# Splitting attention and delta-rule weights with casting and adding DMAs, and adaLN products of attention on VectorE, in a two-layer hybrid decoder

## The chip, the cores and the metric

One core of a Trainium2 chip runs the kernel. The metric is the device time of one execution in microseconds (us). The engines are TensorE (PE, with its weight loads shown apart as PEld), VectorE (DVE), ScalarE (ACT), GpSimd (POOL) and SyncE (SP). Each engine runs its own queue of instructions strictly in order, so an instruction that waits holds up everything behind it on its engine. DMAs are issued by SP, ACT or POOL, each from its place in that engine's queue.

## The reference

What is computed, for 512 positions of width 1024 and two layers:

```python
cond = silu(c)
for layer in range(2):
    mod = cond @ ada_w[layer] + ada_b[layer]
    shift_m, scale_m, gate_m, shift_f, scale_f, gate_f = split(mod, 6)
    h = rmsnorm(x, norm_mix_g[layer]) * (1 + scale_m) + shift_m
    if layer % 2 == 0: mixed = attention_head_groups(h, positions, attn_w_in, attn_w_out)
    else:              mixed = gated_deltanet(h, gdn_w_in, conv_w, a_log, dt_bias, norm_g, gdn_w_out)
    x = x + gate_m * mixed
    h = rmsnorm(x, norm_ffn_g[layer]) * (1 + scale_f) + shift_f
    x = x + gate_f * ((silu(gate) * up) @ ffn_w_out[layer])   # gate, up = split(h @ ffn_w_in[layer])
return rmsnorm(x, final_norm_g)
```

Attention has 8 block-sparse softmax heads with rotary positions and 8 stick-breaking heads, all of 64 columns. The gated delta rule has 8 heads of 128 columns: a short convolution on q, k and v, a triangular system solved in each chunk, and a scan over chunks.

## The kernel before

Everything is float32. A large product is made from three passes of TensorE: weight and activation are each split into a high part, rounded to the type fp32r, and a low part, the rest; the product is high by high, plus high by low, plus low by high. So every weight tile of 128x1024 floats (512 KB) must be split before TensorE can use it.

`fetch` loads the next tile of a fixed list (`weight_plan`) and splits it. SP issues the load into one of three buffers called `raw`; then `split` (lines 246 to 251) writes `wh`, the rounded copy, and `wl = raw - wh`. A letter in the plan names the engines: "a" copies on ACT and subtracts on DVE, "p" copies on ACT and subtracts on POOL, "g" copies on POOL and subtracts on DVE. There are two buffers each of `wh` and `wl`. `load_w` asks for tiles two ahead of the one in use. A projection tile feeds 24 matmuls of 512 columns; two tiles of the projection z of the delta rule feed 48 matmuls of 256 columns in each of two passes.

The letters before: attention's 12 tiles of q and k projections (`EA`) "g"; its four tiles of v (`EVA`) "a"; of the delta rule, k (`EK`) "g", q and v (`EQ`, `EV`) "p", the first half of z (`EZ`) "p" and the second half (`EZ2`) "g".

adaLN: a column of `mod` is the sum of a row tile `aw` (128x1024, loaded by SP into two buffers) times `cond`. With `AENG = "g"` the 24 tiles that fall into attention (`ADA`, six with each of the first four heads) are multiplied on POOL (line 211) and summed on ACT (line 212). All others are one instruction of DVE (line 214).

A scheduler orders the instructions of all engines from dependencies and its own estimate of durations; the program text sets priorities only. The stages follow one another: start with the first projections (0 to 62 us), attention with the other projections between its heads (62 to 313), output projection and first feed-forward (313 to 718), the delta rule (718 to 1050), second feed-forward (to the end). In the delta rule, POOL gathers diagonal blocks (`UC`), writes them to DRAM and reads them back in another shape (`dr1`), DVE inverts them in 31 steps (lines 991 and 993, tiles `DT` and `vp`), and POOL moves the result back the same way (`dr2`); then TensorE finishes the inverse (lines 1016 to 1041) among the matmuls of z (lines 1096 to 1098), and the scan follows.

Of the kernel before, what the change touches and what calls it, by code (L numbers as in the profile page):

```python
# [8 lines left out]
F32 = mybir.dt.float32  # L9
F32R = mybir.dt.float32r  # L10
BF16 = mybir.dt.bfloat16
I32 = mybir.dt.int32
AF = mybir.ActivationFunctionType
OP = mybir.AluOpType
# [46 lines left out]
NEARLY = 14  # L61
LATE = (3, 1)
ORDER = (0, 4, 1, 5, 2, 6, 3, 7)
EK, EQ, EV, EZ, EZ2 = 'g', 'p', 'p', 'p', 'g'
EA, EVA = 12 * 'g', 'aa'
NL = (2, 1)
OG, NG = (6, 8), 18
GS = 4
ROT = 2
NPOOL = 2  # L70
AENG = "g"
ADA = (6, 6, 6, 6, 0, 0, 0, 0)
NSPLIT = 4
NFIRST = 2
NFIRST_GDN = 2


def weight_plan(I):

    p = []

    def add(key, src, kc=KC, n=128, eng="a", keep=False):
        p.append((key, src, kc, n, eng, keep))

    def out(name, src, nsplit, parts, keep, spare=()):
        order = list(range(KC - nsplit)) + (1 if keep or spare else 2) * list(range(KC - nsplit, KC))
        for n in order:  # L90
            for a, b in parts:
                add((name, n, a), src[n][:, a:b], b - a,
                    keep="h" if n in spare else keep and n >= KC - nsplit)

    def ffn(l):
        first = [j + f for f in range(NFIRST) for j in (0, FC)]
        for j in first + [j + f for f in range(NFIRST, FC) for j in (0, FC)]:
            add(("ffn_in", l, j), I["ffn_in"][l, j], keep=j in first)
        out(("ffn_out", l), I["ffn_out"][l], NL[l], ((0, 8), (8, 16), (16, 22)), False, (7,) if l else ())

    def vproj(name, i, eng="a"):
        for j in (0, 4):
            add((name, i, j), I[name][i][:, j:j + 4], 4, 256, eng)

    for k in range(KC):
        add(("attn_first", k), I["attn_first"][k])
    vproj("attn_v", 0, EVA[0])
    vproj("attn_v", 1, EVA[1])
    for i in range(12):
        add(("attn_in", i), I["attn_in"][i], eng=EA[i])  # L110
    out("attn_out", I["attn_out"], NSPLIT, ((0, 8),), True)
    ffn(0)
    first = list(range(8, 8 + NFIRST_GDN))
    for i in 2 * first + list(range(8 + NFIRST_GDN, 16)):
        add(("gdn_in", i), I["gdn_in"][i], eng=EK)
    for i in range(8):
        add(("gdn_in", i), I["gdn_in"][i], eng=EQ)
    for i in range(16, 24):
        add(("gdn_in", i), I["gdn_in"][i], eng=EV)
    for i in range(4):  # L120
        vproj("gdn_z", i, EZ)
    for i in range(4):
        vproj("gdn_z", i, EZ2)
    for i in range(2):
        for n in range(KC):
            add(("gdn_out", n, 0), I["gdn_out"][n])
    ffn(1)
    return p


def build(nc, tc, I, O):
    V, G, A, PE = nc.vector, nc.gpsimd, nc.scalar, nc.tensor
    from contextlib import ExitStack
    ctx = ExitStack()
    with ctx:
        const = ctx.enter_context(tc.tile_pool(name="const", bufs=1))
        res = ctx.enter_context(tc.tile_pool(name="res", bufs=1))
        wpool = ctx.enter_context(tc.tile_pool(name="wpool", bufs=1))
# [104 lines left out]
        def split(src, h, l, eng="a"):  # L243
            ins = None
            if eng in "ap":
                ins = A.activation(h, src, AF.Copy)  # L246
            elif eng == "g":
                G.tensor_scalar(h, src, 1.0, 1.0, op0=OP.mult, op1=OP.mult)  # L248
            else:
                V.tensor_copy(h, src)  # L250
            (G if eng == "p" else V).tensor_tensor(l, src, h.bitcast(F32), op=OP.subtract)  # L251
            return ins


        plan = weight_plan(I)
        loaded, dmas, spare = [], [], []
        used = [0]
        ahead = [0]
        kctx = [None]
        kpool = [None]  # L260
# [3 lines left out]
            kpool[0] = kctx[0].enter_context(tc.tile_pool(name="keep", bufs=1, side="right", reuse_waits="tile"))  # L264


        def fetch():
            _, dram, kc, n, eng, keep = plan[len(loaded)]
            raw = wpool.tile([128, kc, n], F32, name="raw", tag="raw", bufs=3)
            dmas.append(nc.sync.dma_start(raw, dram).ins)  # L270
            if keep == "h":

                w = [[], []]
                for j in range(0, kc, 4):
                    m = min(4, kc - j)
                    t = [x.rearrange("p (a b) -> p a b", b=n)[:, :m] for x in spare.pop(0)]
                    split(raw[:, j:j + m], *t, eng)
                    for i in range(2):
                        w[i] += [t[i][:, k:k + 1] for k in range(m)]
                loaded.append(w)  # L280
                return
            pool, bufs = (kpool[0], 4) if keep else (wpool, 2)
            h = pool.tile([128, kc, n], F32R, name="wh", tag="wh", bufs=bufs)
            l = pool.tile([128, kc, n], F32R, name="wl", tag="wl", bufs=bufs)
            split(raw, h, l, eng)
            loaded.append((h, l))

        def load_w(key):
            i = used[0]
            assert plan[i][0] == key, (plan[i][0], key)  # L290
            while len(loaded) < min(i + 1 + ahead[0], len(plan)):
                fetch()
            used[0] += 1
            w, loaded[i] = loaded[i], None
            return w
# [215 lines left out]
def attention(e, x0ctx):  # L511
    nc, tc, V, G, A, PE, I = e.nc, e.tc, e.V, e.G, e.A, e.PE, e.I
    from contextlib import ExitStack
    with ExitStack() as ctx:
# [271 lines left out]
        for p in range(4):  # L786
            qa, ka, qb, kb = cur
            for h in range(2):
                steps.append([])
                moba(p, h, qa, ka)  # L790
                for j in range(sum(ADA[:2 * p + h]), sum(ADA[:2 * p + h + 1])):
                    with tc.issue_after(e.dmas[KC - 1]), tc.issue_after(sin[1].ins):
                        e.ada(0, 2 + j // 8, j % 8, eng=AENG[j % len(AENG)])
                stick(p, h, qb, kb)
# [495 lines left out]
```

## Time and profile before

| | us |
|---|---|
| median of 3 runs | 1452.05 |
| lowest and highest run | 1450.31, 1454.83 |
| the profiled execution | 1451.28 |
| its span in the profile | 1449.4 |
| PE busy | 1392.6 |
| DVE busy | 879.5 |
| ACT busy | 583.2 |
| POOL busy | 403.6 |

The profiled execution is 1.9 us longer than its span and 0.8 us shorter than the median. A busy time is the sum of an engine's instructions in the profile; instructions that wait, branch or issue DMAs are not in it. A group's row gives its line, engine, operation and tiles, how often it ran, its busy time and the mean of one, and the idle time just before it with what ended it. PEclk is the clock granted to TensorE as a share of its full 2.4 GHz; the other level is half of that.

### The profile page before, as it was taken

The page shows a single profiled execution, that of the slowest core. Times are in us where ns is not written, and L with a number is a line of the kernel's source. Part 1 is how long each engine was busy: PE and PEld are TensorE (multiplying, and loading weights), DVE is VectorE, ACT ScalarE, POOL GpSimd, SP SyncE. Part 2 cuts the span into 40 slices and gives each one's busy share as a digit, 9 for nine tenths or more (in the row PEclk, how much of TensorE's full clock was granted, in tenths as well). Part 3 has the DMA queues.
Part 4 walks back from the last instruction along what each step waited for, and adds up shares of the span by engine and source line. Part 5 has one row for each costly group of instructions (what it writes and reads, how often), then busy time and mean ns, then how long its engine had stood idle before and what let it go on. Part 6 is the DMA issues. An engine that isn't in the chain of part 4 may idle for free.

```text
span 1449.4 us, 19833 instructions
## 1 busy us (share of the span) xinstructions
PE 1392.6 (96%) x7610; PEld 1190.9 (82%) x7610; DVE 879.5 (61%) x1416; ACT 583.2 (40%) x1141; POOL 403.6 (28%) x368
## 2 busy tenths in 40 slices
PE   8888899999999999999999999999999999999997
PEld 5677778879888888888878777999998888888887
DVE  7588887656576676533777898757783433433233
ACT  4466666754222222222456733346562222222222
POOL 4868853212211111011424734332111000000010
PEclk9989999999999999999999999999999999999999
DMA  9445411032276677534622323223361233233332
GB/s 370 157 150 158 143 64 43 30 134 99 81 249 231 217 247 232 163 114 122 184 89 74 76 70 110 66 88 117 104 203 59 88 102 102 87 102 95 91 100 79
DMA packets 57009, 184.47 MB, mean 127 GB/s; under 512 B 6761, under 2 KB 11113, under 8 KB 56914
## 3 DMA queue, kind: packets, MB, share of 16 engines
q1 hardware_dynamic: 55104, 179.91, 38.1%
q0 software_dynamic: 656, 2.23, 0.7%
q8 instruction: 60, 0.98, 0.3%
q10 hardware_dynamic: 1154, 1.05, 0.2%
q14 instruction: 35, 0.29, 0.1%
HBM read 177.88 MB, written 5.29 MB: 126 GB/s over the span
## 4 chain that ended last, share of the span: by engine, by line
PE 75%; DVE 11%; ACT 4%; DMA 3%; POOL 3%; issue 3%; SPq 0%; DVEq 0%; POOLq 0%; ACTq 0%
PE mm L310 19%; PE mm L312 19%; PE mm L311 19%; DVE wl L251 1%; DVE vp L993 1%; PE mm L1097 1%; PE mm L1098 1%; PE mm L1096 1%; PE z L775 1%; DMA vp<-dr 1%; PE f L310 1%; PE f L311 1%; POOL aw L211 1%; PE f L312 1%; DMA aw<-in_ada_w_dram 1%
## 5 line engine op out<-in xcount | busy, mean ns | idle before, releaser
L246 ACT ACTIVATE wh<-raw 128x1024 fp32r<-128x1024 f32 (+1 forms) x199 | 206.8, 1040 | 520.1 <-PE mm L311 384.3
L251 DVE TENSOR_TENSOR wl<-raw,wh 128x1024 fp32r<-128x1024 f32 (+1 forms) x205 | 265.0, 1293 | 218.6 <-ACT wh L246 205.9
L310 PE MATMUL mm<-hh,wh 128*128 128x512 f32 (+1 forms) x776 | 294.1, 379 | 2.4 <-DVE acc L884 2.4
L312 PE MATMUL mm<-hh,wl 128*128 128x512 f32 (+1 forms) x776 | 293.1, 378 | 1.7 <-DVE wl L251 1.7
L311 PE MATMUL mm<-hl,wh 128*128 128x512 f32 (+1 forms) x776 | 293.2, 378 | 0.0
L312 PEld LDWEIGHTS mm<-hh,wl 128*128 128x128 f32 x776 | 148.1, 191 | 28.4 <-DVE wl L251 2.5
L310 PEld LDWEIGHTS mm<-hh,wh 128*128 128x128 f32 x776 | 148.3, 191 | 26.6 <-DVE acc L884 2.6
L311 PEld LDWEIGHTS mm<-hl,wh 128*128 128x128 f32 x776 | 148.3, 191 | 24.2
L248 POOL TENSOR_SCALAR ah<-ac 128x512 fp32r<-128x512 f32 x36 | 40.6, 1128 | 336.8 <-DVE ac L472 336.8
L312 PE MATMUL mm<-ah,wl 128*128 128x512 f32 (+1 forms) x354 | 126.4, 357 | 1.2 <-DVE wl L251 1.2
L310 PE MATMUL mm<-ah,wh 128*128 128x512 f32 (+1 forms) x354 | 125.9, 356 | 0.0
L311 PE MATMUL mm<-al,wh 128*128 128x512 f32 (+1 forms) x354 | 125.9, 356 | 0.0
L310 PE MATMUL mm<-h1h,wh 128*128 128x512 f32 x320 | 124.5, 389 | 0.0
L311 PE MATMUL mm<-h1l,wh 128*128 128x512 f32 x320 | 124.5, 389 | 0.0
L312 PE MATMUL mm<-h1h,wl 128*128 128x512 f32 x320 | 124.5, 389 | 0.0
L472 DVE TENSOR_TENSOR ac<-sg,mm 128x512 f32<-128x512 f32 x40 | 27.5, 688 | 129.4 <-PE mm L312 129.4
L214 DVE CUSTOM_DVE_ANT_0 aw<-aw,cond 128x1024 f32<-128x1024 f32 x72 | 94.8, 1339 | 5.8 <-DMA aw<-in_ada_w_dram 5.6
L330 POOL TENSOR_TENSOR ssq<-ssq,sq 128x512 f32<-128x512 f32 x14 | 22.7, 1624 | 210.9 <-ACT sq L326 210.9
L312 PEld LDWEIGHTS mm<-ah,wl 128*128 128x128 f32 x354 | 66.9, 189 | 11.0 <-DVE wl L251 1.6
L311 PEld LDWEIGHTS mm<-al,wh 128*128 128x128 f32 x354 | 66.9, 189 | 9.5
L310 PEld LDWEIGHTS mm<-ah,wh 128*128 128x128 f32 x354 | 66.9, 189 | 9.3
L251 POOL TENSOR_TENSOR wl<-raw,wh 128x1024 fp32r<-128x1024 f32 x24 | 58.8, 2450 | 43.5 <-ACT wh L246 43.3
(407 smaller groups left out, 2838.3 us busy)
## 6 DMA issues: line engine op xcount, KB each, us to landing
aw<-in_ada_w_dram SPq DMA_DIRECT2D x96, 512.0 KB
raw<-in_ffn_in_dram SPq DMA_DIRECT2D x88, 512.0 KB
raw<-in_ffn_out_dram SPq DMA_DIRECT2D x36, 512.0 KB
raw<-in_gdn_in_dram SPq DMA_DIRECT2D x26, 512.0 KB
raw<-in_gdn_z_dram SPq DMA_DIRECT2D x16, 512.0 KB
raw<-in_gdn_out_dram SPq DMA_DIRECT2D x16, 512.0 KB
raw<-in_ffn_out_dram SPq DMA_DIRECT2D x18, 384.0 KB
raw<-in_attn_in_dram SPq DMA_DIRECT2D x12, 512.0 KB
```

The lines of the kernel that those rows point to most:

```text
L211: ins = G.tensor_tensor(w, w, cond, op=OP.mult)
L214: return V.tensor_tensor_reduce(w, w, cond, 1.0, 0.0, OP.mult, OP.add, mod[:, j:j + 1])
L246: ins = A.activation(h, src, AF.Copy)
L248: G.tensor_scalar(h, src, 1.0, 1.0, op0=OP.mult, op1=OP.mult)
L251: (G if eng == "p" else V).tensor_tensor(l, src, h.bitcast(F32), op=OP.subtract)
L310: PE.matmul(ps, wh[k][:, 0], xh[:, cs], start=first and k == order[0], stop=False)
L311: PE.matmul(ps, wh[k][:, 0], xl[:, cs], start=False, stop=False)
L312: PE.matmul(ps, wl[k][:, 0], xh[:, cs], start=False, stop=last and k == order[-1])
L330: eng.tensor_tensor(ssq[:, cs], ssq[:, cs], sq[:, cs], op=OP.add)
L472: ins = V.tensor_tensor(ac, sg, pu, op=OP.mult)
L775: PE.matmul(o, m, x, start=False, stop=i == len(mms) - 1, skip_group_check=True)
L993: V.tensor_tensor(DV[:, :m, m:], DV[:, :m, m:], d, op=OP.subtract)
```

## The change

52 tiles no longer go through `raw`, SP and two engines. With the new letter "d" POOL issues a DMA from DRAM into `wh`, which rounds on the way; ACT writes `wl = -wh`; and POOL issues a second DMA that reads the same tile from DRAM again and adds it onto `wl`. The 52 are attention's 12 tiles of q and k, its last two of v, and of the delta rule 6 of k, 8 of q, 8 of v and all 16 of z. The first four k tiles of the delta rule become "a". Every third of the "d" tiles takes two of the three `raw` buffers as its pair, so three pairs go around. `AENG` becomes "v": the 24 products of attention are made on DVE by line 214.

```diff
-EK, EQ, EV, EZ, EZ2 = 'g', 'p', 'p', 'p', 'g'
-EA, EVA = 12 * 'g', 'aa'
+EK, EK2, EQ, EV, EZ, EZ2 = 'a', 'd', 'd', 'd', 'd', 'd'
+EA, EVA = 12 * 'd', 'ad'
-AENG = "g"
+AENG = "v"
...
-    for i in 2 * first + list(range(8 + NFIRST_GDN, 16)):
-        add(("gdn_in", i), I["gdn_in"][i], eng=EK)
+    for j, i in enumerate(2 * first + list(range(8 + NFIRST_GDN, 16))):
+        add(("gdn_in", i), I["gdn_in"][i], eng=EK if j < 2 * NFIRST_GDN else EK2)
...
+        def w_pair(keep, kc, n, turn=False):
+            if turn:
+                turns[0] += 1
+            tags = (("raw", 3),) * 2 if turn and turns[0] % 3 == 0 else (("wh", 2), ("wl", 2))
+            return [kpool[0].tile([128, kc, n], F32R, name=t, tag=t, bufs=4) if keep else
+                    wpool.tile([128, kc, n], F32R, name=t, tag=tag, bufs=bufs)
+                    for t, (tag, bufs) in zip(("wh", "wl"), tags)]
...
             _, dram, kc, n, eng, keep = plan[len(loaded)]
+            if eng == "d":
+                h, l = w_pair(keep, kc, n, True)
+                dmas.append(nc.gpsimd.dma_start(h, dram).ins)
+                A.activation(l, h.bitcast(F32), AF.Copy, scale=-1.0)
+                nc.gpsimd.dma_start(l, dram, accum_op=OP.add)
+                loaded.append((h, l))
+                return
```

Lines of the changed kernel past this point stand 17 higher (643 becomes 660, 991 becomes 1008); the two DMAs are its lines 283 and 285, the negation is line 284.

The scheduler orders the program anew. The first place is POOL at the start of attention, when the rotary tables are done (`r`, `rs` and `S` belong to them; `aw` are adaLN tiles). Before:

```order
58 L555 TENSOR_SCALAR r_338<-r_338 128x32
59 L211 TENSOR_TENSOR aw_917<-aw_917,cond_90 128x1024
60 L211 TENSOR_TENSOR aw_921<-aw_921,cond_90 128x1024
61 L643 TENSOR_TENSOR rs_638<-rs_638,S_130 128x512
62 L211 TENSOR_TENSOR aw_925<-aw_925,cond_90 128x1024
63 L211 TENSOR_TENSOR aw_929<-aw_929,cond_90 128x1024
64 L643 TENSOR_TENSOR rs_651<-rs_651,S_130 128x512
65 L211 TENSOR_TENSOR aw_933<-aw_933,cond_90 128x1024
```

Now:

```order
58 L572 TENSOR_SCALAR r_338<-r_338 128x32
59 L283 DMA wh_1240<-in_attn_in_dram 128x1024
60 L660 TENSOR_TENSOR rs_638<-rs_638,S_130 128x512
61 L285 DMA wl_1241<-in_attn_in_dram 128x1024
62 L660 TENSOR_TENSOR rs_651<-rs_651,S_130 128x512
63 L283 DMA wh_1407<-in_attn_in_dram 128x1024
64 L283 DMA wh_706<-in_attn_v_dram 128x1024
```

The products have left POOL, and the loads of attention's last v tiles (`wh_706`) now stand behind the second rotary product (`rs_651`).

The second place is POOL in the delta rule where the diagonal blocks (`vp_6564`, now `vp_6524`) go to DRAM (`dr1`) and come back. Before:

```order
249 L971 TENSOR_SCALAR vp_6564<-uv_6924 32x128 x4
250 L251 TENSOR_TENSOR wl_7701<-raw_7698,wh_7700 128x1024
251 L971 TENSOR_SCALAR vp_6564<-uv_6939 32x128 x4
252 L980 DMA dr1_6346<-vp_6564 128x32x32
253 L1072 TENSOR_TENSOR q4_6326<-qraw_7696,eg_7754 128x512
254 L251 TENSOR_TENSOR wl_7768<-raw_7765,wh_7767 128x1024
255 L981 DMA vp_7049<-dr1_6346 128x1024
```

Now:

```order
255 L285 DMA wl_7715<-in_gdn_in_dram 128x1024
256 L997 DMA dr1_6308<-vp_6524 128x32x32
257 L283 DMA wh_7780<-in_gdn_in_dram 128x1024
258 L1089 TENSOR_TENSOR q4_6288<-qraw_7646,eg_7703 128x512
259 L998 DMA vp_7003<-dr1_6308 128x1024
260 L1003 MEMSET vp_7006 128x1024
261 L1089 TENSOR_TENSOR q5_6289<-qraw_7712,eg_7769 128x512
262 L1004 MEMSET vp_7006 128x32
263 L283 DMA wh_7988<-in_gdn_in_dram 128x1024
264 L285 DMA wl_7847<-in_gdn_in_dram 128x1024
265 L285 DMA wl_7781<-in_gdn_in_dram 128x1024
```

The subtractions have left POOL. In their place stand the DMAs, and the second DMA of the tile `wh_7780` (`wl_7781`) stands behind the read of the blocks, which waits for `dr1` to land.

The third place is POOL in the delta rule's z projection (`gz0`, `gz1` are the gates made of it). Before:

```order
276 L1103 TENSOR_TENSOR gz1_8274<-gz1_8274,rows_6339 128x256
277 L1103 TENSOR_TENSOR gz0_8273<-gz0_8273,rows_6339 128x256
278 L251 TENSOR_TENSOR wl_8346<-raw_8343,wh_8345 128x1024
279 L251 TENSOR_TENSOR wl_8352<-raw_8349,wh_8351 128x1024
280 L1103 TENSOR_TENSOR gz1_8274<-gz1_8274,rows_6339 128x256
```

Now:

```order
292 L1120 TENSOR_TENSOR gz1_8212<-gz1_8212,rows_6301 128x256
293 L285 DMA wl_8280<-in_gdn_z_dram 128x1024
294 L1120 TENSOR_TENSOR gz0_8211<-gz0_8211,rows_6301 128x256
295 L283 DMA wh_8411<-in_gdn_z_dram 128x1024
296 L285 DMA wl_8285<-in_gdn_z_dram 128x1024
297 L283 DMA wh_8345<-in_gdn_z_dram 128x1024
298 L1120 TENSOR_TENSOR gz1_8212<-gz1_8212,rows_6301 128x256
```

Where one subtraction a tile stood, two DMAs a tile stand now; each waits in POOL's queue, the first until TensorE has read the buffer's former tile, the second until ACT has written the negative.

## Rows read from the trace of the kernel before

**Rows 1.** The page's first two parts: busy time, share of the span and instructions of the engines, and PE's granted clock in 40 slices of 36 us.

```profile
PE 1392.6 (96%) x7610; PEld 1190.9 (82%) x7610; DVE 879.5 (61%) x1416; ACT 583.2 (40%) x1141; POOL 403.6 (28%) x368
...
PEclk9989999999999999999999999999999999999999
```

**Rows 2.** Busy time by stretch. Columns: the stretch, its length, then for PE, PEld, DVE, ACT and POOL busy us and number of instructions, then the granted clock, the DMA engines' share and GB/s. 62 to 313 is attention, 450 to 500 the feed-forward, 736 to 1002 the delta rule.

```profile
62.00:97.00 35.00, 26.21 (x149) 23.39 (x148) 23.67 (x42) 22.25 (x52) 22.51 (x10) 0.85 0.43 140
97.00:164.00 67.00, 58.94 (x317) 49.14 (x316) 57.40 (x80) 42.67 (x108) 53.22 (x34) 0.90 0.47 150
164.00:295.00 131.00, 127.42 (x730) 106.42 (x728) 101.36 (x192) 88.38 (x222) 59.64 (x58) 1.00 0.19 61
295.00:313.00 18.00, 14.78 (x59) 10.47 (x58) 9.50 (x15) 11.92 (x22) 0.00 (x0) 0.82 0.20 66
450.00:500.00 50.00, 50.00 (x222) 41.42 (x221) 35.39 (x49) 11.97 (x14) 7.34 (x5) 1.00 0.70 237
736.00:803.00 67.00, 67.00 (x358) 56.87 (x358) 50.65 (x136) 42.28 (x79) 21.84 (x19) 1.00 0.26 84
803.00:901.00 98.00, 89.88 (x439) 74.26 (x437) 83.96 (x142) 44.23 (x89) 52.23 (x48) 0.95 0.30 83
901.00:964.00 63.00, 62.09 (x526) 58.95 (x527) 43.75 (x54) 21.17 (x42) 25.46 (x17) 1.00 0.22 73
964.00:1002.00 38.00, 38.00 (x330) 38.00 (x331) 24.29 (x64) 20.52 (x78) 10.56 (x9) 1.00 0.31 98
```

**Rows 3.** The chain that ended last, 95 to 105 us: start, length, engine, tile and line.

```profile
96.80 3.97 DMA aw<-in_ada_w_dram
...
100.91 2.67 POOL aw L211
...
103.60 1.16 ACT aw L212 x2
...
104.78 2.17 DVE fin L237
```

**Rows 4.** Groups of instructions by form, 62 to 313 us.

```profile
L211 POOL TENSOR_TENSOR aw<-aw,cond 128x1024 f32<-128x1024 f32 x24 | 61.4, 2567 | 21.1 <-DMA aw<-in_ada_w_dram 16.9 <-ACT bh L246 4.2
L248 POOL TENSOR_SCALAR wh<-raw 128x1024 fp32r<-128x1024 f32 x12 | 15.2, 1268 | 11.9 <-PE mm L311 11.9
...
L251 DVE TENSOR_TENSOR wl<-raw,wh 128x1024 fp32r<-128x1024 f32 x21 | 31.8, 1516 | 12.9 <-ACT wh L246 12.3 <-POOL wh L248 0.6
...
L739 DVE TENSOR_SCALAR p<-p,st 128x384 f32<-128x384 f32 x8 | 7.4, 927 | 0.3
...
L212 ACT ACTIVATE aw<-aw 128x1024 f32<-128x1024 f32 x24 | 25.3, 1055 | 9.7 <-POOL aw L211 9.7
L246 ACT ACTIVATE wh<-raw 128x1024 fp32r<-128x1024 f32 x10 | 10.4, 1053 | 3.5 <-PE mm L700 2.8 <-PE mm L311 0.7
```

**Rows 5.** Instructions in order of time, 128 to 132 us, of POOL and of DVE: start, length, line, operation, tiles, shapes, and idle time before.

```profile
128.45 2.41 POOL L211 TENSOR_TENSOR aw<-aw,cond 128x1024 f32<-128x1024 f32 x1
...
128.56 2.45 DVE L739 TENSOR_SCALAR p<-p,st 128x256 f32<-128x256 f32 x1
```

**Rows 6.** The same of POOL and of DVE, 853 to 866 us.

```profile
862.76 2.63 POOL L251 TENSOR_TENSOR wl<-raw,wh 128x1024 fp32r<-128x1024 f32 x1 [5.63 <-ACT wh L246]
...
859.88 0.42 DVE L993 TENSOR_TENSOR vp<-vp,DT 128x255 f32<-128x255 f32 x1
...
863.19 2.48 DVE L993 TENSOR_TENSOR vp<-vp,DT 128x255 f32<-128x255 f32 x1
```

**Rows 7.** Groups of instructions by form: DVE in 0 to 62 us, and POOL and DVE in 736 to 1002 us.

```profile
L214 DVE CUSTOM_DVE_ANT_0 aw<-aw,cond 128x1024 f32<-128x1024 f32 x16 | 19.7, 1243 | 0.0
...
L251 POOL TENSOR_TENSOR wl<-raw,wh 128x1024 fp32r<-128x1024 f32 x24 | 58.8, 2450 | 43.5 <-ACT wh L246 43.3
L248 POOL TENSOR_SCALAR wh<-raw 128x1024 fp32r<-128x1024 f32 x12 | 13.7, 1146 | 44.2 <-PE mm L311 24.7 <-issue 9.6 <-PE mm L1098 8.7
...
L251 DVE TENSOR_TENSOR wl<-raw,wh 128x1024 fp32r<-128x1024 f32 x14 | 18.1, 1295 | 6.1 <-POOL wh L248 5.1 <-ACT wh L246 0.9
L1006 DVE TENSOR_TENSOR uv<-vp,call 128x512 f32<-128x512 f32 x8 | 11.9, 1500 | 7.3 <-PE bank L1033 4.5 <-DMA vp<-dr 2.8
...
L1010 DVE STREAM_TRANSPOSE xinv<-uv 128x512 f32<-128x512 f32 x8 | 5.6, 704 | 0.2
```

**Rows 8.** Instructions in order of time around a 512 KB DMA that POOL issues from DRAM (line 981): POOL and DVE, 823 to 837 us.

```profile
823.64 1.79 POOL L980 DMA_DIRECT2D dr<-vp  x1 [0.30 <-POOL vp L971]
...
830.94 0.62 POOL L981 DMA_DIRECT2D vp<-dr  x1 [1.35 <-DMA dr<-vp]
...
831.02 0.69 DVE L887 SCALAR_TENSOR_TENSOR qraw<-qraw,acc 128x512 f32<-128x512 f32 x1 [0.26 <-ACT qraw L886]
...
835.95 0.41 DVE L991 TENSOR_TENSOR DT<-vp 128x31 f32<-128x31 f32 x1 [2.29 <-DMA vp<-dr]
```

**Rows 9.** Instructions in order of time at the start of attention: POOL's second rotary product, and on DVE the low parts of the last two v tiles.

```profile
79.13 2.27 POOL L643 TENSOR_TENSOR rs<-rs,S 128x512 f32<-128x512 f32 x1
...
93.04 1.23 DVE L251 TENSOR_TENSOR wl<-raw,wh 128x1024 fp32r<-128x1024 f32 x1 [3.14 <-ACT wh L246]
...
95.61 2.09 DVE L251 TENSOR_TENSOR wl<-raw,wh 128x1024 fp32r<-128x1024 f32 x1 [0.25 <-ACT wh L246]
```

More of the change, by code (lines that the diff above doesn't have):

```diff
@@ L264, in open_keep @@
             kpool[0] = kctx[0].enter_context(tc.tile_pool(name="keep", bufs=1, side="right", reuse_waits="tile"))
+        turns = [0]
+        def w_pair(keep, kc, n, turn=False):
[5 more added lines that the diff above has]
+                    for t, (tag, bufs) in zip(("wh", "wl"), tags)]
         def fetch():
             _, dram, kc, n, eng, keep = plan[len(loaded)]
+            if eng == "d":
[5 more added lines that the diff above has]
+                return
             raw = wpool.tile([128, kc, n], F32, name="raw", tag="raw", bufs=3)
@@ L281, in fetch @@
                 return
-            pool, bufs = (kpool[0], 4) if keep else (wpool, 2)
-            h = pool.tile([128, kc, n], F32R, name="wh", tag="wh", bufs=bufs)
-            l = pool.tile([128, kc, n], F32R, name="wl", tag="wl", bufs=bufs)
+            h, l = w_pair(keep, kc, n)
             split(raw, h, l, eng)
```

## The prediction

> **What bounds the kernel now.** I read the busy times first: PE is busy for 1392.6 of 1449.4 us [rows 1], so nothing but PE's idle time and its slow clock can be won. Where that lies is read by stretches [rows 2]. In the feed-forward PE has no idle time and issues 222 matmuls in 50 us, 0.225 us for one of 512 columns; nothing that the change does can help there. In attention PE is idle for 35 - 26.2 = 8.8 us (62 to 97), 67 - 58.9 = 8.1 us (97 to 164) and 131 - 127.4 = 3.6 us (164 to 295), and its clock stands at 0.85 and 0.90 in the first two, which costs 0.15 x 35 = 5.2 and 0.10 x 67 = 6.7 us more: 32 us in all. In the delta rule it is idle for 98 - 89.9 = 8.1 us (803 to 901) and 0.9 us (901 to 964), and the clock of 0.95 costs 0.05 x 98 = 4.9 us: 14 us. The two other stretches there, 736 to 803 and 964 to 1002, are full. So 46 us could be won at the very most, and stretches that are full now can only lose.
>
> What PE waits for in attention shows in the chain: a load of an adaLN tile (3.97), its product on POOL (2.67), its sum on ACT (1.16), and a short DVE instruction (2.17) [rows 3]. These have nothing to do with the heads, but they stand in the queues that the heads use. From 97 to 164 DVE is busy for 57.4 of 67 us and POOL for 53.2 [rows 2]. And DVE's time is not all work. A normalization of `p` takes 2.45 us and ends with POOL's product that started just before it [rows 5]; in the delta rule the same instruction of the same shape takes 0.42 us, and 2.48 us when POOL subtracts beside it [rows 6]. A POOL instruction with two inputs in SBUF holds up DVE for as long as it runs.
>
> **Products to DVE.** Removed: 24 products on POOL at 2.57 us = 61.4 us, 24 sums on ACT = 25.3 us [rows 4]. Added: 24 instructions of line 214 on DVE at 1.24 us [rows 7] = 29.8 us. If each of the 24 products holds up one DVE instruction by 2.48 - 0.42 = 2.06 us, DVE gets 49 us back, if none does, 0; the mean of `p` 128x384 (0.93 us, more than twice the 0.42 us of a like size) says that it is common, so I take half, 25 us.
>
> **Attention's 14 weight tiles.** Removed: 12 POOL copies at 1.27 us and 14 DVE subtractions, 1.23 us undisturbed [rows 4, 9], 17 us. ACT has 12 negations more, at the 1.05 us of its copy of the same size [rows 4], 12.6 us, against 25.3 us that left. POOL has 28 DMA issues more, 0.62 us each [rows 8]. In sum DVE has 25 + 17 - 30 = 12 us less to do, POOL some 60 us less, ACT 13 us less. Of the 32 us I take 14: 60% of the 14.8 us of 97 to 164 (9 us), where this work stands; a quarter of the 14 us of 62 to 97 (3.5 us), since the new order puts the load of the last v tiles behind the second rotary product, which runs at 79.1 to 81.4: with the chain priced below they are split at 81.4 + 11 = 92.4 us, and before it was 94.3 and 97.7 [rows 9]; and 1.5 us of 164 to 295. Bounds: 25 us if nearly all of the first three stretches but the start is won; 4 us if the in-order waits of ACT and POOL for landings take the rest.
>
> **What a tile costs now.** Nothing in the trace rounds or adds on the way, so the price comes from the nearest row: a 512 KB DMA that POOL issues at 830.94 is there at 835.9, 4.9 us [rows 8]. One tile is a chain: buffer free, first DMA 4.9, negation 1.05, second DMA at least 4.9: 11 us. Before, only the copy and the subtraction stood behind a free buffer (1.05 + 2.45 [rows 7]), since `raw` was loaded ahead. Bounds: 9 us, with the 3.97 us of a load from SP [rows 3] for both DMAs; 16 us, if the adding DMA, which reads its destination as well, takes twice 4.9. I take 11, the row itself.
>
> A rule speaks of the price too. The Trainium skill, "DMA: Bandwidth & Descriptors", section "Anatomy of one DMA — SWDGE (gpsimd) path", gives 2.0 us plus bytes over 436 GB/s for a DMA of GpSimd; an estimate by it is 3.2 us for 512 KB, and the chain would be 7.5 us. The row says 4.9 with other loads beside it, and the measured number decides.
>
> **The delta rule's 38 tiles.** Removed: 24 POOL subtractions, 58.8 us, 12 POOL copies, 13.7 us, and 14 DVE subtractions, 18.1 us [rows 7]. Those subtractions stretch DVE too: `uv` of line 1006 takes 1.50 us where a transpose of the same size takes 0.70 [rows 7], and the 31 steps on DVE lose about 2 us wherever they meet one [rows 6]. DVE is busy for 84 of 98 us in 803 to 901, where PE waits. Of the 14 us I take 9; bounds 3 and 13. ACT's copies become negations at the same price. What the first four k tiles cost as "a" is covered by ACT's idle time (42.3 of 67 us busy).
>
> Against that stand the chains. With three pairs of buffers a tile's chain has to fit between the last matmul that reads a pair and the first that needs the next tile in it. In q and v, where a tile feeds 24 x 0.225 = 5.4 us of matmuls, two tiles and their neighbours' other matmuls lie between, 11.8 us or more: 11 fits, 14 costs about 6 us over the tiles, 16 about 15 us. In z it doesn't fit: two tiles are in use at once and one pair is left. Counted in the new order of PE, at 38 / 330 = 0.115 us a matmul [rows 2], six tiles have 71, 88, 64, 66, 78 and 77 matmuls: 8.2, 10.1, 7.4, 7.6, 9.0 and 8.9 us. A stall before a tile also delays its need, so neighbours share it (the second with the third, the fifth with the sixth). With 11 us the stalls are 2.8, 0.9, 2.7, 3.4, 2.0 and 0: 12 us. With 9 us they are 4 us, with 14 us 24, with 16 us 31. PE is full there now (62.1 of 63 and 38 of 38 us), so nothing hides them.
>
> One more place is POOL's queue at `dr1`: `wl_7781` stands behind the read of the blocks, which waits for the write to land, 7.3 us after its issue [rows 8]. Its first DMA overlaps that wait, the second does not: 0 to 5 us, I take 3.
>
> **The sum.** -14 - 9 + 12 + 3 = -8 us. The profiled execution took 1451.3, so 1443.3; the median of the runs is 0.8 us above that execution: 1444.
>
> **The rivals.** First, slower: the adding DMA is long. If its data takes 3 us more than a copy's, the chain is 14 us, z loses 24, q and v 6: -14 - 9 + 24 + 6 + 3 = +10, 1462; at 16 us it is 1477. It decides from a chain of about 12.6 us on. For it: the add reads twice what a copy reads. Against it: the copy's 4.9 us are mostly not data. Chance 0.22.
>
> Second, also slower: POOL's DMAs are slowed by DVE. Each issue would wait for the DVE instruction that runs, up to 1.24 us [rows 7], twice a tile: 11 + 2.5 = 13.5 us, z loses 21 and q and v 5, 1458. The row speaks against it: the issue at 830.94 took 0.62 us with a DVE instruction of two SBUF inputs beside it [rows 8]. Chance 0.05. By the Trainium skill, "SBUF — State Buffer", section "SBUF: two separate sides", GpSimd cannot write descriptors while DVE runs an instruction in a two-port mode; the trace shows no such wait at the one issue that could have met it.
>
> Third, no change: DVE's relief isn't what PE waits for, since the 24 products stand in DVE's queue before and among the first head's softmax, each behind the load of its tile, and the heads wait as before. Attention then gives 6 us and z takes them: 1451. For it: DVE stays over 70% busy there ((57.4 - 9) of 67 us). Chance 0.17.
>
> Fourth, more: the chain takes 9 us or less and attention returns 20 us: -20 - 9 + 4 + 1 = -24, 1428. Chance 0.16.
>
> **How the numbers follow.** The forecast has 0.40. Faster is forecast and fourth, 0.56; within 0.3% (4.4 us, about what a measurement of this kernel can tell from no change) is the third, 0.17; slower 0.27. The range reaches down to 1424, between the fourth and the bounds of all gains (-25 - 13 + 4 + 0 = -34), and up to 1470, past the first rival at 14 us; less than 2 in 10 are left out.
>
> **What would show it.** DVE's stretched instructions gone from 97 to 164 and from 840 to 875, `p` 128x384 near 0.5 us; PE's idle time in attention down by a third or more; and in the z projection PE waiting in lines 1113 to 1115 for a DMA into `wl`, some 3 us at a time. Landings of the second DMA above 7 us after issue, or PE waiting for them in q and v, would make the first rival true. Wrong would be the whole picture if the z stretch stayed full, or if the heads' waits for DVE stayed as long with POOL empty.

## The result, and the profile after

The changed kernel takes 1473.59 us at the median of three executions (1470.81 to 1473.67), the kernel before 1453.13 beside it: a ratio of 1.0137, 95% interval 1.0111 to 1.0163, some 20 us slower. Executions at a far lower clock are left out of every time, one here and one of e3_gdn_only below, which was the one that was profiled there. The forecast was 1444, the range 1424 to 1470; both the side and the range were missed. The profiled execution took 1473.67 us, with a span of 1471.8.

The page of the changed kernel, busy times:

```profile
PE 1395.9 (95%) x7610; PEld 1194.7 (81%) x7610; DVE 820.2 (56%) x1436; ACT 587.6 (40%) x1123; POOL 318.0 (22%) x394
```

DVE has 59 us less to do and POOL 86 [rows 1], as was meant, and yet PE's idle time grew from 57 to 76 us. Where, the stretches tell (same columns as [rows 2]):

```profile
62.00:97.00 35.00, 24.32 (x137) 22.04 (x135) 28.84 (x62) 15.91 (x38) 9.03 (x12) 0.85 0.65 195
97.00:164.00 67.00, 58.92 (x335) 50.37 (x335) 45.18 (x101) 35.20 (x87) 25.14 (x30) 0.90 0.75 212
164.00:295.00 131.00, 127.49 (x728) 107.42 (x726) 87.66 (x182) 90.76 (x219) 43.11 (x56) 0.99 0.30 69
803.00:901.00 98.00, 91.07 (x461) 75.12 (x460) 72.44 (x156) 49.91 (x101) 38.78 (x60) 0.97 0.65 145
901.00:1022.00 121.00, 106.15 (x843) 100.51 (x841) 52.16 (x112) 49.54 (x128) 32.32 (x42) 0.94 0.65 144
```

Attention is as it was, with half of POOL's work gone. The last stretch, z, was 101 us long and full; now it is 121 us, with 15 us idle and a granted clock of 0.94 on the mean, so that part of it ran at 1.2 instead of 2.4 GHz: up to 0.06 x 121 = 7 us more. The first such piece begins in an idle stretch:

```profile
899.00:903.00 4.00, 3.85 (x18) 2.93 (x16) 2.79 (x5) 2.65 (x4) 3.17 (x3) 1.00 0.21 31
903.00:909.00 6.00, 0.00 (x0) 0.00 (x0) 3.46 (x6) 0.00 (x0) 0.53 (x1) 0.71 1.01 211
909.00:915.00 6.00, 5.68 (x37) 5.68 (x38) 2.94 (x5) 3.40 (x5) 1.75 (x2) 0.72 0.60 164
```

While PE stands still there, the 16 DMA engines are full (1.01) and move 211 GB/s; with the same engines the feed-forward moves 237 GB/s at 0.70 [rows 2]. Two of PE's waits of 718 to 1022 us (total, times, longest), and then the DMA view of 803 to 1022 us (POOL's queue with packets, MB and share; issues, KB each, median us from issue to landing):

```profile
PE mm L1114 <- DMA wl<-in_gdn_z_dram: 13.2, 6, 6.5
PE f L327 <- ACT hh L396: 2.8, 2, 2.5
```

```profile
q0 software_dynamic: 8352, 30.41, 63.2%
...
wh<-in_gdn_z_dram POOLq DMA_DIRECT2D x16, 512.0 KB, 6.7
wl<-in_gdn_z_dram POOLq DMA_DIRECT2D x16, 512.0 KB, 6.7
wl<-in_gdn_in_dram POOLq DMA_DIRECT2D x11, 512.0 KB, 5.7
wh<-in_gdn_in_dram POOLq DMA_DIRECT2D x10, 512.0 KB, 5.0
```

A z tile's chain is 6.7 + 1.06 + 6.7 = 14.5 us, not 11. The queues stretch it: POOL's part of z, in order of time,

```profile
911.91 1.81 POOL L285 DMA_DIRECT2D wl<-in_gdn_z_dram  x2 [8.35 <-ACT wl L284]
915.88 0.55 POOL L283 DMA_DIRECT2D wh<-in_gdn_z_dram  x1 [2.15 <-PE mm L1115]
923.57 0.85 POOL L285 DMA_DIRECT2D wl<-in_gdn_z_dram  x1 [7.14 <-ACT gz L1117]
```

shows POOL waiting 7 to 8 us before an adding DMA for its negation, which waits for the first DMA (in the third row the profile names `gz`, which ACT makes right behind that negation).

To place gains and losses, I take the time at which PE begins its n-th us of work, less n: its delay. Each matmul counts at its duration in full stretches (0.227 us for 512 columns, 0.120 for 256, and so on, 1333 us in sum in every kernel). The delay that each stage adds, in us, from the profiled executions (0 to 290 ends with attention, 290 to 640 is the feed-forward, 640 to 650 the start of the delta rule, 650 to 790 holds k, q and most of v, 790 to 905 the last v tiles and z):

```
kernel         0-290  -640  -650  -790  -905   end   all
before          75.2   2.4   4.3  15.9   3.7  15.2  116.6
changed         75.0   2.4   7.8  13.6  25.1  15.0  139.0
e1_z_old        70.2   2.5   7.7  14.3   9.8  15.2  119.6
e2_attn_only    71.9   2.4   4.3  17.3   2.8  15.5  114.3
e4_aeng_only    63.3   2.4   4.3  15.8   3.7  14.9  104.5
e5_attn_v_aa    73.1   2.4   4.3  15.8   3.7  15.6  114.9
e6_copy         64.5   2.4   7.8   7.0   8.1  15.0  104.8
e7_pairs4       75.1   2.5   8.1  15.8  23.9  14.8  140.0
e8_gdn_a        63.9   2.4   4.3  10.9  11.1  14.9  107.5
e9_k_a          63.7   2.4   3.9  19.0   2.4  15.2  106.6
e10_sum_act     62.9   2.5   4.3  19.4   2.4  15.1  106.5
e11_q_a         62.9   2.4   4.3  16.2   6.1  14.7  106.7
e12_z_only      62.8   2.4   4.3  17.8  20.9  16.9  125.0
```

The changed kernel loses 21.4 us in the stage of the last v tiles and z and 3.5 at the start of the delta rule, wins 2.3 in k, q and v, and wins nothing in attention. Of the 21.4 us, 6.1 are lost in e1_z_old as well, whose z is split as before; z's own DMAs cost the other 15.3 (17.2 in e12_z_only, where z alone has them).

Part of the 6.1 stands at `dr2`. POOL can issue the read of `dr2` only when its write has landed, and that took 3.0 us before, 7.9 in e1_z_old and 10.6 in the changed kernel, where the write was issued at 888.01. The read on POOL, before and now (`vp<-dr`; the profile names no releaser for the 8.57 us):

```profile
889.88 1.72 POOL L996 DMA_DIRECT2D vp<-dr  x1
```

```profile
899.83 1.72 POOL L1013 DMA_DIRECT2D vp<-dr  x1 [8.57 <-issue]
901.53 0.92 POOL L285 DMA_DIRECT2D wl<-in_gdn_z_dram  x1
```

DVE makes `xinv` from it for the rest of the inverse, and in e1_z_old PE waits 3.1 us for that (0.7 before),

```profile
PE bank L1033 <- DVE xinv L1027: 3.1, 1, 3.1
```

and in the changed kernel the first DMAs of z stand behind the read. This is read from the rows and was not tried.

### The profile page after: what moved, and what is told of

The parts are those of the page before. It is cut to its first block, busy times and chain, and to the rows that moved or that the text cites. A ratio compares the mean times of both kernels' runs of the same rounds, so it can differ in the third digit from the quotient of the medians.

```text
span 1471.8 us, 19830 instructions
## 1 busy us (share of the span) xinstructions
PE 1395.9 (95%) x7610; PEld 1194.7 (81%) x7610; DVE 820.2 (56%) x1436; ACT 587.6 (40%) x1123; POOL 318.0 (22%) x394
## 3 DMA queue, kind: packets, MB, share of 16 engines
q1 hardware_dynamic: 47616, 152.65, 31.3%
q0 software_dynamic: 15632, 56.77, 17.3%
## 4 chain that ended last, share of the span: by engine, by line
PE 72%; DMA 10%; DVE 6%; issue 5%; ACT 4%; POOL 4%; SPq 0%; POOLq 0%; DVEq 0%; ACTq 0%
PE mm L329 19%; PE mm L327 19%; PE mm L328 19%; DMA wl<-in_gdn_z_dram 2%; DMA wh<-in_gdn_in_dram 2%; DVE wl L251 1%; DMA aw<-in_ada_w_dram 1%; DVE aw L214 1%; PE z L792 1%; DMA wh<-in_gdn_z_dram 1%; PE f L328 1%; PE f L329 1%; PE f L327 1%; DMA wl<-in_gdn_in_dram 1%; PE o L729 1%
## 5 line engine op out<-in xcount | busy, mean ns | idle before, releaser
L246 ACT ACTIVATE wh<-raw 128x1024 fp32r<-128x1024 f32 x177 | 183.5, 1039 | 505.3 <-PE mm L328 379.8
L251 DVE TENSOR_TENSOR wl<-raw,wh 128x1024 fp32r<-128x1024 f32 x177 | 225.4, 1275 | 204.8 <-ACT wh L246 201.6
L328 PEld LDWEIGHTS mm<-hl,wh 128*128 128x128 f32 x776 | 146.7, 189 | 23.9
L214 DVE CUSTOM_DVE_ANT_0 aw<-aw,cond 128x1024 f32<-128x1024 f32 x96 | 124.5, 1314 | 15.9 <-DMA aw<-in_ada_w_dram 15.8
L284 ACT ACTIVATE wl<-wh 128x1024 fp32r<-128x1024 f32 x52 | 54.5, 1056 | 103.6 <-DMA wh<-in_gdn_in_dram 41.3
L328 PEld LDWEIGHTS mm<-h1l,wh 128*128 128x128 f32 x320 | 60.1, 188 | 12.5
```

The lines of the kernel that those rows point to most:

```text
L214: return V.tensor_tensor_reduce(w, w, cond, 1.0, 0.0, OP.mult, OP.add, mod[:, j:j + 1])
L284: A.activation(l, h.bitcast(F32), AF.Copy, scale=-1.0)
L328: PE.matmul(ps, wh[k][:, 0], xl[:, cs], start=False, stop=False)
```

## Experiments

Ratios are to the kernel before, measured on the same chip in the same hours (1451.6 to 1452.6 us). Letters that a diff doesn't name are those of the kernel it is made from.

**Parts of the change.** e1_z_old is the changed kernel with

```diff
-EK, EK2, EQ, EV, EZ, EZ2 = 'a', 'd', 'd', 'd', 'd', 'd'
+EK, EK2, EQ, EV, EZ, EZ2 = 'a', 'd', 'd', 'd', 'p', 'g'
```

> The changed kernel with only the 16 z tiles back on the old letters (first half copied on ACT and subtracted on POOL, second half copied on POOL and subtracted on DVE). Theory: the change loses in z alone what it loses (PE's delay grows by about 22 us there), so this kernel comes to 1473.6 - 22 = 1452, 1448 to 1456, and no wait of PE for a DMA into wl is left in the z lines. Rival: the added DMAs cost wherever they run (57 MB more or less through one queue, POOL's issues, DVE and ACT waiting for them), z being only the place where the delay appears; then half or more of the loss stays: 1462 or more.

Measured: 1453.21 us, 1.0016 (1.0005 to 1.0028). The time returns 20 us, as the first theory says. By the table 15.3 of them are z's and 4.8 come from attention, whose instructions and their order are the same in both kernels; so not all of the 20 us are shown to be z's, and 6.1 us stay in the same stage without its DMAs.

e2_attn_only has attention as changed and the delta rule as before:

```diff
-EK, EK2, EQ, EV, EZ, EZ2 = 'a', 'd', 'd', 'd', 'd', 'd'
+EK, EK2, EQ, EV, EZ, EZ2 = 'g', 'g', 'p', 'p', 'p', 'g'
```

> Only the attention half of the change: 14 tiles split by DMAs and the 24 products on VectorE; the delta rule has its old letters. Theory: attention gave nothing, since what the heads won (about 14 us between 100 and 170 us) only paid for the late v tiles, so 1453, 1449 to 1457. Rival: attention gave the 14 us of the prediction and the delta rule costs 34 us and more instead of 20: 1439.

Measured: 1448.93 us, 0.9981 (0.9971 to 0.9990). Attention gives 3 us, not 14. With e1_z_old, k, q and v by DMAs cost 1453.2 - 1448.9 = 4 us.

e3_gdn_only is its counterpart, with `EA, EVA = 12 * 'g', 'aa'` and `AENG = "g"` in the changed kernel.

> Only the delta-rule half of the change: k, q, v and z split by DMAs; attention as before. Theory: all of the loss is here, 1453 + 20 = 1473, 1469 to 1477. Rival: the delta rule costs 34 us and more: 1487.

Measured: 1482.71 us at the median of three executions (1475.65 to 1486.26), 1.0209 (1.0174 to 1.0243), by the interval 25 to 35 us more than before. That is nearer to the rival, and at or above what the other parts leave for this half (1473.6 - 1448.9 = 25 us). No row tells why; this stays open.

e4_aeng_only keeps the old letters everywhere and takes over one line:

```diff
-AENG = "g"
+AENG = "v"
```

> The kernel before with one edit: the 24 products of attention on VectorE, no tile split by a DMA. Theory: POOL's products hold up VectorE and with it the heads, and no v tile comes late here, so attention gives 7 to 14 us: 1439 to 1446. Rival: PE's delay after 160 us is set by something both kernels share (the loads of the adaLN tiles, ACT), so that it stood at 54 us in both; then 1453, 1449 to 1457.

Measured: 1439.87 us, 0.9923 (0.9907 to 0.9940). It beats both kernels. 12 us come back in attention and nothing changes elsewhere. Its page and stretches:

```profile
PE 1383.3 (96%) x7610; PEld 1185.4 (82%) x7610; DVE 879.9 (61%) x1464; ACT 560.2 (39%) x1093; POOL 344.7 (24%) x344
```

```profile
62.00:97.00 35.00, 24.83 (x146) 21.79 (x144) 29.05 (x60) 17.25 (x41) 6.56 (x8) 0.90 0.61 196
97.00:164.00 67.00, 63.08 (x367) 54.64 (x368) 58.90 (x120) 32.93 (x87) 25.81 (x22) 0.95 0.53 175
```

DVE's busy time is that of before to within 0.4 us [rows 1], although it now makes the 24 products (23 of them in this group's 30.3 us): it lost as much elsewhere.

```profile
L214 DVE CUSTOM_DVE_ANT_0 aw<-aw,cond 128x1024 f32<-128x1024 f32 x23 | 30.3, 1319 | 6.7 <-DMA aw<-in_ada_w_dram 6.6
L756 DVE TENSOR_SCALAR p<-p,st 128x384 f32<-128x384 f32 x8 | 5.8, 720 | 0.3
```

**What eats it in attention.** So attention's DMA splits cost the 9 us between e2_attn_only and e4_aeng_only. e5_attn_v_aa is e2_attn_only with the v tiles as before:

```diff
-EA, EVA = 12 * 'd', 'ad'
+EA, EVA = 12 * 'd', 'aa'
```

> The attention half alone as in e2_attn_only, but the last two v tiles back on the old letter (through SP, ACT and VectorE); q and k still by DMAs. Theory: the 9 us between e4_aeng_only and e2_attn_only are the last v tiles, which GpSimd's queue loads behind the second rotary product; then 1440, 1437 to 1443. Rival: they are the chains of the q and k tiles; then 1449 as in e2_attn_only.

Measured: 1450.18 us, 0.9992 (0.9983 to 1.0002). The theory falls: with the v tiles as before the loss stays, so the q and k tiles bring it by themselves.

**The adding itself.** e6_copy is the changed kernel with one argument gone. It leaves out the addition, so `wl` holds the whole weight and not its low part:

```diff
-                nc.gpsimd.dma_start(l, dram, accum_op=OP.add)
+                nc.gpsimd.dma_start(l, dram)
```

> The changed kernel with the second DMA of all 52 tiles copying instead of adding, so that wl holds the whole weight and not its low part; everything else as it was. Theory: the adding DMA, which reads its destination too, is longer than a copying one, and z's chain shrinks with it: landings of wl in z fall from 6.7 us to 5 or less, the time to 1467 or less. Rival: any 512 KB DMA of GpSimd costs the DMA engines as much, and what stretched the landings is that two run at once: 1472 to 1475 and landings as before.

Measured: 1439.54 us, 0.9915 (0.9899 to 0.9931). All engines run the same instructions in the same order as in the changed kernel, and still 34 us are gone: 10.5 in attention, 6.6 in k, q and v, 17.0 in the last v tiles and z. This decides the study: the chains, the queues and the in-order waits are all still there, and only the addition is not. (With it goes about 0.3 us of each issue on POOL, 0.89 against 0.55 us in z; the run does not tell this apart from the transfer itself.) Its DMA view of the same piece of the program (793 to 991 us) and PE's wait for z:

```profile
q0 software_dynamic: 8064, 29.36, 50.7%
...
wh<-in_gdn_z_dram POOLq DMA_DIRECT2D x16, 512.0 KB, 5.0
wl<-in_gdn_z_dram POOLq DMA_DIRECT2D x16, 512.0 KB, 4.8
```

```profile
PE mm L1114 <- DMA wl<-in_gdn_z_dram: 3.3, 2, 2.5
```

The chain is 5.0 + 1.06 + 4.8 = 10.9 us. The first DMA was not touched, and its landing fell from 6.7 to 5.0 as well. The DMA queues of the two pages, changed and copying:

```profile
q1 hardware_dynamic: 47616, 152.65, 31.3%
q0 software_dynamic: 15632, 56.77, 17.3%
```

```profile
q1 hardware_dynamic: 47616, 152.65, 32.3%
q0 software_dynamic: 15632, 56.77, 13.2%
```

For the same packets and bytes POOL's queue holds the 16 engines for 0.173 x 1471.8 = 254.6 us against 0.132 x 1437.6 = 189.8: 65 us more, 1.25 us for each of the 52 adding DMAs. A copying one of 512 KB takes about 189.8 x 0.524 / 56.77 = 1.75 us of them, so an adding one about 3.0.

In attention, 5.3 of the 10.5 us are PE's waits for a `wl` of a DMA, one of a v tile and one of a q or k tile, which e6_copy does not have (waits of the changed kernel, 62 to 300 us):

```profile
PE mm L716 <- DMA wl<-in_attn_v_dram: 3.1, 1, 3.1
PE mm L329 <- DMA wl<-in_attn_in_dram: 2.2, 1, 2.2
```

The other half is the clock: from 62 to 97 and 97 to 164 us it stands at 0.90 and 0.95 in e6_copy, against 0.85 and 0.90, so that more of the changed kernel's time runs at 1.2 GHz; that is 0.05 x 102 = 5 us.

e6_copy (1439.5 us, 0.9915) also ends where e4_aeng_only does (1439.9, 0.9923). So even without the addition the DMA splits return no more than that one line does by itself.

**Buffers.** e7_pairs4 gives z a fourth pair (the third `raw` buffer, and two idle `sq` buffers for the halves of `wl`); the core of it:

```diff
+            if zturn[0] and turn:
+                zturn[0] += 1
+                if zturn[0] % 4 == 0:
+                    return (wpool.tile([128, kc, n], F32R, name="wh", tag="raw", bufs=3),
+                            [wpool.tile([128, 2, n], F32R, name="wl", tag="sq", bufs=3) for _ in range(2)])
+                turns[0] = 3 if zturn[0] % 4 == 2 else 1
```

> The changed kernel with a fourth pair of buffers for the z tiles (the third raw buffer for wh, two idle sq buffers for the halves of wl, so every fourth tile has two negations and two adding DMAs of half the size). Theory: what costs in z is that a tile's chain of 14 us starts only when the last pass but one has let go of its pair; with a fourth pair it starts a pass earlier, PE's waits for wl fall from 28 us (13 waits of PE and PEld) to under 10, and the time to 1458, 1453 to 1463. Rival: the queues of GpSimd and ACT, in which the tiles' steps wait for one another in order, or the DMA engines set the pace; then PE's waits stay above 20 us and the time above 1467.

Measured: 1470.91 us, 1.0123 (1.0101 to 1.0146). The theory falls. PE waits less often for `wl` (its line 1128),

```profile
PE mm L1128 <- DMA wl<-in_gdn_z_dram: 8.6, 2, 6.3
```

and with its weight loads its waits for `wl` fall from 13.2 + 15.2 = 28.4 to 8.6 + 9.1 = 17.7 us, between the theory and the rival. But the stage adds 23.9 us against 25.1: the missing pair costs 1 us there, and 3 in the times. This fits a pace that is set ahead of the buffers.

**No DMA in the delta rule.** e8_gdn_a is e4_aeng_only with the subtractions on DVE:

```diff
-EK, EK2, EQ, EV, EZ, EZ2 = 'g', 'g', 'p', 'p', 'p', 'g'
+EK, EK2, EQ, EV, EZ, EZ2 = 'g', 'g', 'a', 'a', 'a', 'g'
```

> e4_aeng_only with q, v and the first half of z of the delta rule copied on ACT and subtracted on VectorE instead of GpSimd: no DMA splits, but GpSimd's 24 subtractions are gone as they are in the changed kernel. Theory: each subtraction on GpSimd holds up one VectorE instruction by 2 us, so VectorE pays 24 x 1.25 = 30 us for its own subtractions and gets most of 49 us back, and PE wins 2 to 9 us: 1431 to 1438. Rival: the hold-ups cost PE nothing and VectorE's added work does, since it stands in the 98 us where VectorE is 86% busy: 1442 to 1448.

Measured: 1440.77 us, 0.9925 (0.9908 to 0.9942), the same as e4_aeng_only. It lies between the two theories: up to the last v tiles PE wins 4.9 us, and behind them it loses 7.4, with one wait for a convolution on DVE:

```profile
PE mm L327 <- DVE acc L901: 4.1, 1, 4.1
```

e11_q_a moves only q's subtractions (`EQ = 'a'`, the rest as in e4_aeng_only).

> e4_aeng_only with only the eight q tiles of the delta rule subtracted on VectorE instead of GpSimd. In e8_gdn_a PE won 5 us up to the v tiles and lost 6.5 at the last v tile, where it waited 4 us for a convolution on VectorE. Theory: the gain belongs to q and the loss to v, whose subtractions stand among the 31 steps of the inversion: 1435, 1433 to 1437. Rival: gain and loss are the same work moved along VectorE's queue: 1440, 1438 to 1442.

Measured: 1441.36 us, 0.9926 (0.9911 to 0.9941). The rival holds: relief for DVE that DVE pays for itself is none for PE.

**The first four k tiles.** e9_k_a is e4_aeng_only with `EK = 'a'`.

> e4_aeng_only with one edit: the first four k tiles of the delta rule on letter a (copied on ACT instead of GpSimd), as in the changed kernel, and no DMA splits. In every kernel with DMA splits in the delta rule PE is 3.5 us later after its start (it waits 2.7 us for ACT's rounding of the normalized input). Theory: ACT's queue holds the first negation there, which waits for its DMA (2.5 us), and the rounding stands behind it; without that DMA the four tiles cost nothing: 1440, 1438 to 1442. Rival: ACT's four copies themselves delay the rounding, against the prediction: 1443.5.

Measured: 1440.94 us, 0.9923 (0.9908 to 0.9938); the start of the delta rule adds 3.9 us, against 4.3 in e4_aeng_only and 7.8 in the changed kernel. The copies are free. What is left is the negation, in the changed kernel's ACT queue in order of time:

```profile
721.83 1.06 ACT L284 ACTIVATE wl<-wh 128x1024 fp32r<-128x1024 f32 x1 [2.49 <-DMA wh<-in_gdn_in_dram]
722.79 0.49 ACT L396 ACTIVATE hh<-sq,fin 128x256 fp32r<-128x256 f32 x1
```

It waits 2.5 us for its DMA, and the rounding of the normalized input, for which PE waits (the 2.8 us above), stands behind it. This was read, not tried.

**What relieved attention.** e10_sum_act is e4_aeng_only with the product plain and the sum back on ACT:

```diff
-            if eng == "g":
-                ins = G.tensor_tensor(w, w, cond, op=OP.mult)
+            if eng in "gs":
+                ins = (G if eng == "g" else V).tensor_tensor(w, w, cond, op=OP.mult)
```

with `AENG = "s"`.

> e4_aeng_only with the 24 products of attention on VectorE by a plain product, and their sums on ACT as before the change. Theory: the 12 us come from VectorE, which GpSimd's products held up; they stay although ACT has its 25 us of sums back: 1439 to 1443. Rival: they come from ACT, rid of 24 sums that each waited for a product and held the heads' exponentials behind them: 1448 or more.

Measured: 1442.04 us, 0.9938 (0.9922 to 0.9955). With ACT as loaded as before, the gain stays, 10 of 12 us by the medians: it comes from taking the products off POOL. It isn't ACT's waiting for products either, which was 9.7 us before [rows 4] and is longer now:

```profile
L212 ACT ACTIVATE aw<-aw 128x1024 f32<-128x1024 f32 x24 | 25.4, 1058 | 16.4 <-DVE aw L211 15.7 <-DVE st L755 0.5
```

The group of the probabilities of [rows 4] (0.93 us there) is now

```profile
L756 DVE TENSOR_SCALAR p<-p,st 128x384 f32<-128x384 f32 x8 | 3.4, 431 | 0.2
```

**z alone.** e12_z_only is e4_aeng_only with `EZ, EZ2 = 'd', 'd'`.

> e4_aeng_only with z alone split by DMAs. Theory: z's tiles cost 20 us by themselves, since each follows the one before at the pace of a landing and a negation: 1460, 1456 to 1464. Rival: a good part of z's delay is the backlog that q and v leave in GpSimd's queue; alone z costs 12 us or less: 1452 or less.

Measured: 1462.52 us (1457.58 to 1471.51, a wide spread), 1.0077 (1.0047 to 1.0107), 23 us above e4_aeng_only. The theory holds. Its landings, 880 to 1000 us:

```profile
wl<-in_gdn_z_dram POOLq DMA_DIRECT2D x16, 512.0 KB, 6.1
wh<-in_gdn_z_dram POOLq DMA_DIRECT2D x15, 512.0 KB, 5.2
```

No backlog of q and v is needed for most of z's loss.

## Why the prediction was wrong

**The step that failed is the price of a tile**: "Nothing in the trace rounds or adds on the way, so the price comes from the nearest row", 4.9 us for either DMA, 11 us for the chain. The first rival, an adding DMA that is long, was the one that came true; it was given 0.22. The measured chain in z is 14.5 us, inside the bounds of 9 and 16, and e6_copy, whose second DMA only copies, has the chain of 10.9 us that was priced and takes 1439.5, 4.5 us from the forecast. So the forecast fits the kernel that it priced, and the addition is all that stands between that kernel and this one: 34 us. That it fits so well is in part luck: in e6_copy attention gives 11 us where 14 were taken, z costs 4 where 12 were, and the first negation costs 3.5 where nothing was, and these misses cancel.

The same step failed a second time in attention. The chain there has about the price that was worked out (4.4 + 1.06 + 5.5 = 11.0 us by the medians), but no loss was entered for it, and the addition alone costs 10.5 us there (5.7 to 10.6 by the four kernels that share this code).

**Why it is long.** The row that was taken is a copy. By e6_copy an adding DMA holds the DMA engines for 3.0 us where a copying one holds them for 1.75, and it lengthens the DMAs beside it: `wh`, which adds nothing, lands 1.7 us later. The packet records of the trace show the unit: a packet of 4 KB takes 174 ns in the median of POOL's queue in e6_copy; in the changed kernel about half take 174 and half 328. The Trainium skill, "Collectives: The Full Stack", section "The bandwidth ceiling: the fold count and why AG ≠ RS ≠ AR", says of another path that an addition on the way is slow because it needs two source reads, not because adding costs time. The 328 against 174 ns, 1.9 times, agree with two reads; no run here tells reading from adding. The prediction had this argument among those for its rival and set against it that "the copy's 4.9 us are mostly not data". That was true of a copying DMA alone (1.75 of 4.9 us), and left out that several are under way at once, where the data of one is the wait of the next. The 3.2 us estimated by the Trainium skill, "DMA: Bandwidth & Descriptors", section "Anatomy of one DMA — SWDGE (gpsimd) path", lie below all median landings of these weight tiles, 3.9 to 5.5 us in e6_copy and 4.4 to 8.2 in the changed kernel. With other DMAs beside, the measured number was the better one, and still too small for z.

**Term by term** (changed kernel and e6_copy, from the table of delays):
- Attention, -14 (bounds -4 and -25): 0 in the changed kernel's profile, -3 as measured in e2_attn_only, -11 in e6_copy. The products alone gave -12 in e4_aeng_only. DVE's hold-ups that went with them are about its 30 us of new products, since its busy time stayed; 25 had been taken. In the changed kernel the group of `p` 128x384 has 0.61 us (0.93 in [rows 4]; "near 0.5" was said). The weight tiles' part was wrong in sign, as said above. It was said that the last v tiles would be split at 92.4 us; in the changed kernel their adding DMAs are issued at 101.1 and 105.4, and PE waits for them, 2.0 us for a `wh` and 3.1 for a `wl`. e5_attn_v_aa shows that without this the loss is the same.
- Delta-rule relief, -9 (with q and v fitting at 11 us): -8.9 in e6_copy, stage 650 to 790, and -2.3 in the changed kernel. The prediction's 6 us for q and v would make up for that, but they stand for a chain of 14 us, and the chain there is 5.0 + 1.06 + 5.7 = 11.8 by the medians, for which it had no loss. PE waits there 1.0 us for a `wl` of a DMA and some 2 us more for DVE than in e6_copy; the rest stays open. The reading that POOL's subtractions stretch DVE was right: `uv` 128x512, 1.50 us in [rows 7], takes 0.78 in the changed kernel.
- The z chains, +12 at 11 us and 24 at 14: +4.4 in e6_copy at 10.9, +17.2 in e12_z_only at 5.2 + 1.06 + 6.1 = 12.4, +21.4 in the changed kernel at 14.5, of which 15.3 are z's by e1_z_old. A longer chain costs more than the copying one, as worked out, but from 12.4 to 14.5 us no growth of z's own part is shown. That a pair of buffers is what lacks was wrong: a fourth gave 1 us (e7_pairs4). Rather one tile follows another at a landing and a negation, 6.7 + 1.06 = 7.8 us against 48 x 0.115 = 5.5 us of matmuls, since its first DMA stands in POOL's queue behind the other's wait for ACT; with a copying DMA it is 5.0 + 1.06 = 6.1 us. This is argued from the rows of POOL's queue and was not tried.
- First four k tiles, nothing: right for the copies (e9_k_a). The first negation behind them, 3.5 us in the changed kernel and in e6_copy, was not in the sum: of ACT only the idle time was read, not what stands in its queue behind a wait.
- `dr1` in POOL's queue, +3: not to be told apart within its stage. The landing of its write rose from 7.0 to 8.8 us (7.9 in e6_copy). That of `dr2`, for which the sum has no term, rose more, from 3.0 to 10.6 (6.8 in e6_copy), with z's first DMAs behind it.

By the prediction's own numbers, with the chains as measured, 14.5 us in z and 11.8 in q and v, the sum is -14 - 9 + 26 + 0 + 3 = +6; the table has 139.0 - 116.6 = +22. The 16 us between are attention (14), the negation (3.5) and k, q and v (7), less 8 that z, its neighbours and `dr1` cost less than their 26 + 3. So the right length of z's chain would not have given the time: the cost of the same DMAs in attention was missing.

The rivals: the sign given for the first, landings above 7 us, came only in part (6.7 at the median in z, up to 9.9), and it was true all the same. That DVE delays POOL's issues is not the cause, as e6_copy has the same DVE work beside the same issues, and each of its 52 second DMAs is issued in 0.53 to 0.60 us. The row that the prediction held against this rival could not decide it: the DVE instruction of [rows 8] began 0.08 us after the issue, and DVE stood idle when the issue began. The third, that attention's relief isn't what PE waits for, is refuted by e4_aeng_only; the fourth, a chain of 9 us, did not come.

## What to carry to other kernels

Price an operation that the trace doesn't hold by what it does to the shared resource (bytes read and written, on engines that others use too), not by the landing of the nearest lone example; and where a chain decides, put its price into every stage that uses it, attention as well as z. A change of two ideas is worth taking apart before it is judged: here one line was worth 12 us and the rest of the change cost 34. Work taken off an engine helps only if another engine that PE waits for doesn't pay for it in the same stretch (e8_gdn_a, e11_q_a).

## What the hardware showed that was not expected

An adding DMA of 512 KB from DRAM into SBUF costs the 16 DMA engines about 1.7 times a copying one (3.0 against 1.75 us), and a DMA of POOL that rounds costs about a tenth more than a load by SP (1.75 against 0.323 x 1437.6 x 0.524 / 152.65 = 1.59 us). POOL itself is held longer too: the issue of the adding DMA in z takes 0.89 us, that of the copying one in e6_copy 0.55. And attention fed by such splits is less steady: it ends at a delay of 70.2, 71.9, 75.0 and 75.1 us in four kernels that share its code, against 62.8 to 63.9 in the six that have products on DVE and no DMA splits there.
